# A hybrid decoder layer on one core: two products of four units directly behind the keys, and eight operand sums moved to GpSimd

## The chip, the core and the metric

The kernel runs on one core of a Trainium2 chip. A core has a matrix engine (TensorE, PE in the profile; its weight loads are listed as PEld), VectorE (DVE), ScalarE (ACT), GpSimd (POOL) and SyncE (SP), which issues most DMAs. Each engine runs its own instruction stream in order and waits at semaphores for the others. The metric is the device time of one execution in microseconds (us), as the median of several runs.

## The reference

One layer over 2048 tokens of 1024 channels in fp32. The combined projection `w_in` makes convolution inputs, queries, keys, values and gates; a short causal convolution and a sliding-window attention (16 heads of 64, 4 key heads, window 128) run beside each other, and two gated projections and one last projection follow.

```python
h = rms_norm(x, norm_g)
u = jnp.einsum('bsd,dc->bsc', h, w_in)
v_c, b_c, c_c, z_c, q, k, v, z_a, gate_logits = jnp.split(u, SPLIT_POINTS, axis=-1)
...
y_a = jnp.einsum('bsc,cd->bsd', y_c, w_conv_out)
q = rms_norm(q.reshape(b, s, N_Q_HEADS, HEAD_DIM), q_norm_g)
k = rms_norm(k.reshape(b, s, N_KV_HEADS, HEAD_DIM), k_norm_g)
...
o = sliding_window_attention(q, k, v, sinks) * jax.nn.silu(z_a)
y_b = jnp.einsum('bsc,cd->bsd', o, w_attn_out)
gates = jax.nn.sigmoid(gate_logits + gate_b)
g_a, g_b = jnp.split(gates, N_BRANCHES, axis=-1)
merged = g_a * y_a + g_b * y_b
return x + jnp.einsum('bsd,de->bse', merged, w_out)
```

## The kernel before

**Tiles and units.** The tokens are done in two tiles of 1024, each as two halves of 512. The columns of a projection are done in units of 256 (two blocks of 128). A unit is a 2 x 2 block product (two halves of the channels, two halves of the tokens, two column blocks), and it is computed with seven products instead of eight, after Strassen and Winograd. The products are numbered 1 to 7. Product 1 and 2 use the weights as they are (`_a`), 6 and 5 use sums of them (`_s`), 7 and 3 other sums (`_t`) and 4 the single block `_d`. On the side of the tokens, product m uses the operand m: `form(t, m, j)` makes `oph_m_j`, for each of four chunks j of 128 channels pairs. Operands 5, 6, 7 and 4 are of sums of normed inputs, made by `first_sum`, `third`, `second_sum` and `last_sum`; operands 1, 2, 3 are the normed inputs.

**One product.** fp32 is split in a high and a low part (`split`): ScalarE casts the high part (L306 for operands, L466 for weights), VectorE subtracts it to get the low part (every woven VectorE instruction has line L275). A product is for each of four chunks high x high, high x low and low x high: 12 matmuls 128x512 (L639).

**The opening.** In the first tile the keys and values of all tokens come first (`kv_by_token`, L777, 16 ticks). Behind them, the first gate unit (`ga`, 0) is done by `qunit` with the plain eight products (L754), as its operands 1, 2, 3 and 8 are the normed inputs themselves. Then come the four query units `q` 0 to 3 by `sunit`, the convolution units `cv` and `b`, the rest of the gates, `z`, `za` and the output projections.

In `sunit` product 1 goes to a bank X, ScalarE copies X to the bank Y (L657); product 5 goes to a bank V and is copied to `s5` (L666); product 6 is added on Y, and VectorE makes V = s5 + Y. So the order is 1, 5, 6, 2, 7, 3, 4. `spair` does two units product by product. Finished queries are copied (L790), cast (`q_h`, L1073), stored by four GpSimd DMAs to `q2d` (L1078), and transposed by TensorE for the squares of their norm (`ptq`, L913, squared on ScalarE at L996). Finished gates get a tanh (L1417); finished keys (`k_n`, `ksq`, `kss`, `k_h`) a norm with a square root, whose table ScalarE must load.

**What sets the order.** `manual_schedule` keeps every engine's stream as the program writes it. `run` counts one tick per product; in each tick it writes the next weight piece (high cast first, low part behind), then what `put(n, f)` has noted for tick n, then a few woven VectorE steps. The tables of numbers at the top give these ticks: `OPEN_AT` for the operands of the opening, `KV_PLACES` for keys and values, `STEPS_0` and `STEPS_1` for the steps of attention in the two tiles, `WO_SUMS_AT` for the sums of `w_o` (`wo_sums`), which the last projection reads from DRAM (`wsd`). `plan` lists the weight units in the order of use, with a kind: "S" is a seven-product unit with one load of 1 MB, "P" the eight-product one; `piece` gives out their pieces as room in the weight buffers comes free.

**An attention step** `j_b` (key head j, block b of 128 tokens) has the scores `s_j_b` (the bank is first filled with the sinks by ScalarE, L1237; matmuls L1249 and L1252), a softmax, a turn of p to `f` on VectorE and through DRAM (`fd`, L1293; back as `x`, L1300; both issued by GpSimd), casts to `xh` and `yp` (L1307, L1308), a low part `xl`, four selects on GpSimd (L1321), and the values `po_j_b` (L1338).

Of the kernel before, what the change touches and what calls it, by code (L numbers as in the profile page):

```python
# [8 lines left out]
F32 = mybir.dt.float32  # L9
# [6 lines left out]
P = 128  # L16
# [3 lines left out]
H = 512  # L20
# [37 lines left out]

K_AT = (1, 1, 4)

T0_SHIFT = 1
OPEN_AT = (2, 2, 2, 7, 7, 8, 5, 4, 5, 6, 4, 6, 5, 5, 6, 7, 9, 6, 7, 8, 7, 8, 8, 10, 12, 11, 14, 14, 14, 13, 17, 14, 14, 19, 18, 14, 16, 20, 20, 19, 20, 20, 18, 16, 19, 14, 20, 19, 22, 22, 23, 22, 23, 23, 8, 8, 14, 14, 26, 18, 22, 25, 27, 20, 26, 27, 21, 19, 23, 24, 18, 19, 19, 19, 28, 22, 28, 27)
KV_PLACES = (8, 11, 22, 26, 8, 11, 13, 40, 13, 31, 31, 30, 36, 36)
TURNED_AT = (6, 12)

K_ROOT = True
# [14 lines left out]
STEPS_0 = (60, 63, 71, 74, 78, 85, 92, 95, 99, 104, 110, 115, 121, 128, 131, 136, 139, 142, 146, 149, 152, 155, 159, 162, 165, 170, 173, 176, 181, 184, 187, 192)  # L81
# [44 lines left out]
def block_kernel(  # L126
# [281 lines left out]
    def load_half(i=None):  # L408

        if i is None:
            i = next(k for k in range(2 * len(plan)) if k not in raws)
        n, h = divmod(i, 2)
        kind, srcs, key = plan[n]
        if kind == "L":
            raws[i] = None
            return
        if n not in raw_of:  # L420
            raw_of[n] = rawpool.tile(
                [P, 2, 2, H], F32, tag="raw", name="w" + "_".join(str(i) for i in key) + "_raw")
        both = raw_of[n]
        if kind == "R":
            raw = both[:, h]
            for p in range(2):
                nc.sync.dma_start(raw[:, p], srcs[(2 * h + p) * P : (2 * h + p + 1) * P])

                for c in FIRST_X.get((i, p), ()):
                    xt_load(c, 0)  # L430
        elif kind in "SP":
# [12 lines left out]
        raws[i] = raw  # L444
        rawlive[0] += 1
# [11 lines left out]
    def pieces_of(n):  # L457
# [37 lines left out]
        if kind in "SP":  # L495
            def pair(h, m1, m2, nm):
                hi, lo = (v.rearrange("p (i j c) -> p i j c", i=2, c=P) for v in wpair(f"{name}_{nm}"))
                for i, m in enumerate((m1, m2)):
# [2 lines left out]
                return two(hi, lo, raw[:, h] if summed else raw[:, :, h])  # L501

            summed = []

            if kind == "P":
                return w, [(2, 2 * h, lambda h=h: pair(h, (h, 0), (h, 1), f"p{h}")) for h in range(2)]

            def single():
                hl = wpool.tile([P, 2, KP, P], F32R, tag="w", name=f"{name}_d")
# [38 lines left out]
            def second():  # L548
# [3 lines left out]
                for i, m in enumerate((7, 3)):  # L552
# [25 lines left out]
    def open_prep():  # L578
        n = len(ready)
        if n >= len(plan):  # L580
            return False
        if n in paired:
            both = [pieces_of(n + e) for e in range(2)]
            ready.extend(w for w, _ in both)
            todo.extend((n + e, i) + both[e][1][i] for e, i in (PAIR_LOADS if plan[n][0] == "L" else PAIR_PIECES))
            return True
        w, pieces = pieces_of(n)
        ready.append(w)
        todo.extend((n, i) + p for i, p in enumerate(pieces))
        return True  # L590

    def piece():

        if not todo and (len(ready) > used[0] or not open_prep()):
            return None
        n, i, cost, last, f = todo[0]
        if tick[0] < held.get(n, 0):
            return None
        need = [2 * n + i] if plan[n][0] in "TP" else [2 * n, 2 * n + 1][: 1 + min(i, 1)]
# [30 lines left out]

    B_AT = {(0, 0): 1, (1, 0): 2, (0, 1): 8, (1, 1): 3}

    def product(ps, u, n, ops, start):
        force(u, n)
        hi, lo = ready[u][n]
        for j in range(KP):
            b = ops[n][j]
            for i, (w, m) in enumerate(((hi, 0), (hi, 1), (lo, 0))):
                nc.tensor.matmul(  # L639
                    ps, lhsT=w[:, j, :], rhs=b[:, m, :],  # L640
                    start=start and j == 0 and i == 0, stop=j == KP - 1 and i == 2,
                    skip_group_check=not start)
        d = done.setdefault(u, set())
        d.add(n)
        live[0] -= sum(c for m, c in USES if n in m and m <= d)
# [94 lines left out]
    def qunit(key, ops, fin):  # L740


        u = unit(key)
        nm = "_".join(str(i) for i in key)
        for q in range(2):
            for i in range(2):
                ps = bank(f"Q{nm}_{i}_{q}")
                for p in range(2):
                    force(u, (i, p))
                    hi, lo = ready[u][i, p]  # L750
                    for j in range(KP):
                        b = ops[B_AT[p, q]][j]
                        for k, (w, m) in enumerate(((hi, 0), (hi, 1), (lo, 0))):
                            nc.tensor.matmul(  # L754
                                ps, lhsT=w[:, j, :], rhs=b[:, m, :],
                                start=p == 0 and j == 0 and k == 0, stop=p == 1 and j == KP - 1 and k == 2)
                    if p:
                        fin(i, q, ps)
                        live[0] -= 2 * q
                    yield  # L760

    def kv_by_token(places, banks):

# [84 lines left out]
    def norm_l(t, c, st):  # L848
        x_norm(st["raw"][c, 0], c, st["rb"][0])

    def third(c, st):

        raw = st["raw"]
        sub(raw[c - 1, 1], raw[c, 1], raw[c - 1, 1])

    def norm_r(t, c, st):

# [9 lines left out]
        raw = st["raw"]  # L867
        sub(raw[2 * j, 0], raw[2 * j + 1, 1], raw[2 * j, 0])

    def last_sum(j, st, to=None):  # L870

        raw = st["raw"]
        o = st.setdefault("t4", {})[j] = raw[2 * j, 0] if to is None else to
        sub(o, raw[2 * j + 1, 0], raw[2 * j, 0])

    def form(t, m, j, st):
        raw = st["raw"]
# [754 lines left out]
    for t in range(NT):  # L1632
# [9 lines left out]
        else:  # L1642
            at_(("k", t))
            at_(("v", t))
        for j in range(EARLY[t]):
            at_(("ga", t, j))
        for j in range(NKV):
            at_(("q", t, j))
        if t == 0:
            plan[2] = ("P",) + plan[2][1:]  # L1650
        for k in range(KC):
            at_(("cv", t, k))
            if k % 2:
# [148 lines left out]
    put(OPEN_AT[31], lambda: form(0, 8, 1, st))  # L1802
    put(OPEN_AT[32], lambda: form(0, 8, 2, st))
    put(OPEN_AT[33], lambda: form(0, 8, 3, st))
# [25 lines left out]
    put(OPEN_AT[59], lambda: third(3, st))  # L1830
    put(OPEN_AT[60], lambda: third(5, st))
    put(OPEN_AT[61], lambda: third(7, st))
# [123 lines left out]
    for t in range(NT):  # L1956
# [12 lines left out]
        firsts = [(("ga", t, j), fin_g(t, 0, j)) for j in range(EARLY[t])]  # L1969
        firsts += [(("q", t, j), fin_q(t, j)) for j in range(NKV)]  # L1970
        for n, (key, fin) in enumerate(firsts):
            run((qunit if t == n == 0 else sunit)(key, ops, fin))
        for k in range(KC):
            run(sunit(("cv", t, k), ops, fin_cv(t, k, ys)))
            if k % 2:
# [17 lines left out]
        zs += [("za", j) + fin_z(t, j, od[t], "za", use_y) for j in range(NJ)]  # L1993
        zs[0][3]()
        if t + 1 == NT:
            for j in range(KP):
                wo_sums(tick[0] + WO_SUMS_AT[j], j)
        if t == 0:
            for j in range(2):
# [151 lines left out]
```

## Time and profile before

| | us |
|---|---|
| median of 3 runs | 1901.33 (1898.82 to 1902.93) |
| the profiled execution | 1901.07 |
| its span, first to last instruction | 1899.4 |
| TensorE busy | 1888.9 |
| VectorE busy | 1498.6 |
| ScalarE busy | 990.5 |
| GpSimd busy | 608.7 |

The granted TensorE clock is 1.000 over the whole span. A row of the timeline gives the start, the time that it and what is grouped with it took, engine, line, operation, output and inputs, and in brackets the idle time before it with what ended it; two neighbouring starts on an engine tell what one instruction costs there, since the end of one overlaps the next.

### The profile page before, as it was taken

The page shows a single profiled execution, that of the slowest core. Times are in us where ns is not written, and L with a number is a line of the kernel's source. Part 1 is how long each engine was busy: PE and PEld are TensorE (multiplying, and loading weights), DVE is VectorE, ACT ScalarE, POOL GpSimd, SP SyncE. Part 2 cuts the span into 40 slices and gives each one's busy share as a digit, 9 for nine tenths or more (in the row PEclk, how much of TensorE's full clock was granted, in tenths as well). Part 3 has the DMA queues.
Part 4 walks back from the last instruction along what each step waited for, and adds up shares of the span by engine and source line. Part 5 has one row for each costly group of instructions (what it writes and reads, how often), then busy time and mean ns, then how long its engine had stood idle before and what let it go on. Part 6 is the DMA issues. An engine that isn't in the chain of part 4 may idle for free.

```text
span 1899.4 us, 27260 instructions
## 1 busy us (share of the span) xinstructions
PE 1888.9 (99%) x8670; PEld 1572.7 (83%) x8670; DVE 1498.6 (79%) x2364; ACT 990.5 (52%) x1967; POOL 608.7 (32%) x846
## 2 busy tenths in 40 slices
PE   9999999999999999999999999999999999999999
PEld 7888888888887888888888888888888888888887
DVE  7989898887777767668799788887778777787754
ACT  7665455456766443434565455556666434444321
POOL 2073435335655000011372344445656000121000
PEclk9999999999999999999999999999999999999999
DMA  8286555568777957895584655567778887779653
GB/s 299 77 238 177 167 169 167 162 189 245 240 229 226 302 197 245 276 279 130 155 233 128 181 175 154 168 206 228 242 235 256 272 319 274 274 194 264 215 175 110
DMA packets 222495, 402.20 MB, mean 212 GB/s; under 512 B 30032, under 2 KB 104784, under 8 KB 212880
## 3 DMA queue, kind: packets, MB, share of 16 engines
q1 hardware_dynamic: 188224, 313.10, 50.6%
q0 software_dynamic: 30528, 78.94, 15.7%
q10 hardware_dynamic: 3600, 8.42, 1.3%
q8 instruction: 69, 1.13, 0.2%
q14 instruction: 74, 0.61, 0.1%
HBM read 271.09 MB, written 129.25 MB: 211 GB/s over the span
## 4 chain that ended last, share of the span: by engine, by line
PE 65%; DVE 2%; DMA 2%; issue 0%; ACT 0%; SPq 0%; DVEq 0%; ACTq 0%
PE Y L639 24%; PE ya L1479 4%; PE Vcv L639 2%; PE Xcv L639 2%; PE Xyb L639 2%; PE Vo L639 2%; PE Xo L639 2%; PE Vyb L639 2%; PE Vza L639 2%; PE Xza L639 2%; PE Xz L639 1%; PE Vz L639 1%; PE po L1338 1%; PE Vga L639 1%; PE Xgb L639 1%; PE Vgb L639 1%
## 5 line engine op out<-in xcount | busy, mean ns | idle before, releaser
L1300 POOL DMA_DIRECT2D x<-fd x256 | 140.0, 554 | 127.0 <-DMA fd<-f 58.1
L1274 ACT ACTIVATE p<-s,st,rq 128x129 f32<-128x129 f32 x256 | 114.2, 458 | 33.2 <-DVE st L275 21.2
L1321 POOL TENSOR_SCALAR_AFFINE_SELECT xh<-xh 64x512 fp32r<-64x512 f32 x64 | 61.0, 953 | 151.4 <-DVE xl L275 103.2
L1293 POOL DMA_DIRECT2D fd<-f x64 | 37.0, 578 | 194.3 <-DVE f L275 169.0
L1562 POOL DMA_DIRECT2D mt<-tha x16 | 13.8, 863 | 254.9 <-DVE tha L275 236.2
L639 PE MATMUL Xcv<-oph,wcv_ah 128*128 128x512 f32 x256 | 78.9, 389 | 0.0
L1321 POOL TENSOR_SCALAR_AFFINE_SELECT yp<-xl 64x512 fp32r<-64x512 f32 x64 | 72.3, 1130 | 3.1
L1321 POOL TENSOR_SCALAR_AFFINE_SELECT xl<-xl 64x512 fp32r<-64x512 f32 x64 | 67.7, 1058 | 4.4
L1321 POOL TENSOR_SCALAR_AFFINE_SELECT yp<-yp 64x512 fp32r<-64x512 f32 x64 | 57.8, 903 | 4.2
L275 DVE TENSOR_TENSOR o<-po,o 64x256 f32<-64x256 f32 x128 | 53.5, 418 | 5.0 <-ACT o L1350 4.1
L275 DVE SCALAR_TENSOR_TENSOR y<-u,cols,y 128x512 f32<-128x512 f32 x64 | 53.6, 837 | 3.7 <-ACT y L1387 2.5
L639 PEld LDWEIGHTS Xcv<-oph,wcv_ah 128*128 128x128 f32 x256 | 47.8, 188 | 9.4
L275 DVE TENSOR_TENSOR p<-p,st 128x512 f32<-128x512 f32 x64 | 50.4, 787 | 3.4
L275 DVE STREAM_TRANSPOSE f<-p 128x512 f32<-128x512 f32 x64 | 45.5, 711 | 8.5 <-DMA fd<-f 5.6
L466 ACT CAST wcv_sh<-wcv_raw 128x1024 fp32r<-128x1024 f32 x16 | 16.9, 1054 | 67.1 <-DVE wcv_raw L275 67.1
L1274 ACT ACTIVATION_READ_ACCUMULATOR p<-s,st,rq 128x1 f32 x256 | 51.3, 200 | 0.0
L1249 PEld LDWEIGHTS s<-kq,q 128*128 128x128 f32 x256 | 46.1, 189 | 5.8 <-ACT s L1237 1.8
L1078 POOL DMA_DIRECT2D q2d<-q_h x64 | 44.3, 692 | 18.9 <-ACT q_h L1073 7.7
L1350 ACT COPY o<-po 64x256 f32<-64x256 f32 x128 | 47.1, 368 | 6.0 <-DMA wpd_yb<-wph_yb 2.2
L2052 POOL DMA_DIRECT2D oc<-ocd x12 | 6.5, 545 | 136.1 <-ACT ophc L306 130.1
L639 PE MATMUL Xcv<-oph,wcv_al 128*128 128x512 f32 x128 | 49.9, 390 | 0.0
L1078 POOL DMA_DIRECT2D q2d<-q_l x64 | 44.2, 690 | 14.7 <-DMA q2d<-q_h 7.5
(711 smaller groups left out, 6409.1 us busy)
## 6 DMA issues: line engine op xcount, KB each, us to landing
gd<-th SPq DMA_DIRECT2D x64, 256.0 KB, 2.8
wcv_raw<-in_w_units SPq DMA_DIRECT2D x16, 1024.0 KB, 5.5
q<-q2d SPq DMA_DIRECT2D x64, 256.0 KB, 5.4
v<-vd SPq DMA_DIRECT2D x128, 128.0 KB, 3.5
fd<-f POOLq DMA_DIRECT2D x64, 256.0 KB, 4.2
x<-fd POOLq DMA_DIRECT2D x256, 64.0 KB, 3.5
th<-gd SPq DMA_DIRECT2D x48, 256.0 KB, 5.0
wga_raw<-in_w_units SPq DMA_DIRECT2D x8, 1024.0 KB, 5.4
```

Of the source, the lines that this page charges most:

```text
L275: r = f(*args, **kw)
L466: return (lambda: nc.scalar.copy(hi, src), lambda: vec.tensor_tensor(out=lo, in0=src, in1=hi.bitcast(F32), op=ALU.subtract))
L639: nc.tensor.matmul(ps, lhsT=w[:, j, :], rhs=b[:, m, :], start=start and j == 0 and i == 0, stop=j == KP - 1 and i == 2, skip_group_check=n ...
L1078: nc.gpsimd.dma_start(q2d[t][j][half, q * 2 * HB : (q + 1) * 2 * HB, i, e, :], src[HALVES[e]].bitcast(F32).rearrange("p (b x) -> p b x", x ...
L1249: nc.tensor.matmul(sp[:, h, c, skip : 3 * HD], lhsT=q2[:, h, c, :], rhs=kq[:, 0, keys], start=c == 0, stop=False)
L1274: nc.scalar.activation(out=p[:, i, :], in_=sg[:, i, HD : 3 * HD + 1], func=AF.Exp, bias=st[:, 1, i : i + 1], scale=rv[:, i // 2, i % 2 : i ...
L1293: nc.gpsimd.dma_start(fd, f)
L1300: nc.gpsimd.dma_start(x[QUADS[k]], src[k])
L1321: nc.gpsimd.affine_select(out=d4, in_=s4, pattern=[[0, 2], [-32 * sg, 2], [0, G], [-sg, 32]], compare_op=ALU.is_gt if prev else ALU.is_ge, ...
L1338: nc.tensor.matmul(po[:, cs], lhsT=v2[:, kind + h, :], rhs=xx[:, :, h * HD : (h + 1) * HD], start=n == h == 0, stop=n == 2 and h == 1)
L1350: nc.scalar.copy(ov, pov[oth, :, e])
L1479: nc.tensor.matmul(ps, lhsT=w[:, j, cs], rhs=o[:, m, :], start=n == 0 and i == 0, stop=n == KC - 1 and i == 2)
```

## The change

The gate unit `ga` 0 becomes a seven-product unit, and the first four units are done in two pairs, (q 0, ga 0) and (q 1, q 2). Behind the keys stand products 1 and 2 of both pairs (`hpair`): product 1 of the two, then product 2 of the two. Product 1 is copied to an SBUF slot `head` by ScalarE, and product 2 finishes its quarter of the unit. For these products half of each unit's weights is loaded on its own (kind "F", 512 KB a unit, 2 MB in all). Then come products 5, 6, 7, 3 and 4 of the first pair, one unit beside the other, and of the second pair (`rpair`); `head` is copied to Y again behind product 5. For these the unit's whole 1 MB is loaded (kind "M"), as the sums need it. Query unit 3 follows by `sunit` as before.

Operand 8 is no longer made (four casts, four low parts). `third` and `last_sum` of the first tile, four each, run on GpSimd. Operand 3 is made some ticks later. In the first tile attention step 28 (3_4) is put one tick earlier and step 30 (3_6) one later, with `T0_SHIFT` 0 for 1, since the opening has one tick less. The `w_o` sums of chunks 0 and 1 move from `z` of the second tile to its start.

```diff
-T0_SHIFT = 1
+T0_SHIFT = 0
-WO_SUMS_AT = (8, 17, 26, 35)
+WO_SUMS_AT = (5, 13, 8, 44)
+OPENING = ((("q", 0, 0), ("ga", 0, 0)), (("q", 0, 1), ("q", 0, 2)))
+REST = (5, 6, 7, 3, 4)
+REST_HOLD = 5
...
+        elif kind == "F":
+            raw = both[:, h].rearrange("p k (j c) -> p k j c", c=P)
+            src = w_units[unit_index(srcs[h])].rearrange("r (k h x) -> r k h x", k=2, h=2)[:, :, 0]
+            nc.sync.dma_start(both[:, h], src)
...
+            if kind == "M":
+                return w, [(0, 0, sums_first), (2, 0, first), (2, 0, second), (1, 2, single)]
...
+    def hpair(key, ops, subs):
         u = unit(key)
...
+        for e, (sub, _) in enumerate(subs):
+            nm = "_".join(str(i) for i in sub)
+            xbs.append(bank(f"X{nm}"))
+            product(xbs[e], u, 1, ops, True, (e, 1))
+            heads[sub] = slot([P, H], F32, f"head{nm}")
+            nc.scalar.copy(heads[sub], xbs[e])
+            yield
+        for e, (_, fin) in enumerate(subs):
+            product(xbs[e], u, 2, ops, False, (e, 2))
+            fin(0, 0, xbs[e])
+            yield
...
+    def rpair(keys, ops, fins):
...
+        held[us[1] + 1] = tick[0] + REST_HOLD
...
+        for n, e in ((n, e) for n in REST for e in range(2)):
+            u, fin, nm = us[e], fins[e], nms[e]
+            if n == 5:
+                vb[e] = bank(f"V{nm}")
+                product(vb[e], u, 5, ops, True)
+                s5[e] = spare(f"s5{nm}")
+                nc.scalar.copy(s5[e], vb[e])
+                if e:
+                    yb[e] = mbank(f"Y{nm}").rearrange("p b q -> p (b q)")
+                nc.scalar.copy(yb[e], heads.pop(keys[e]))
+            elif n == 6:
+                product(yb[e], u, 6, ops, False)
+                add(vb[e], s5[e], yb[e])
...
-        last_sum(j, st, slot([P, H], F32, f"t4_{j}"))
+        last_sum(j, st, slot([P, H], F32, f"t4_{j}"), nc.gpsimd)
...
-    put(OPEN_AT[30], lambda: form(0, 8, 0, st))
...
-    put(OPEN_AT[58], lambda: third(1, st))
+    put(OPEN_AT[58], lambda: third(1, st, nc.gpsimd))
...
+        if t + 1 == NT:
+            for j in range(2):
+                wo_sums(tick[0] + WO_SUMS_AT[j], j)
         attention(t, [t0 + n for n in (STEPS_0, STEPS_1)[t]])
...
+            for j, pair in enumerate(subs):
+                run(hpair(("f", j), ops, pair))
+            for pair in subs:
+                run(rpair([k for k, _ in pair], ops, [f for _, f in pair]))
```

**VectorE in the opening.** First VectorE's stream before, about the weights of the first query unit's products 5 and 6 (`wq_0_sl`) and its products 7 and 3 (`wq_0_tl`); names `oph_m_j` are low parts of operands, `xt` and `t` are sums.

```order
L275 TENSOR_TENSOR wq_0_sl<-wq_0_raw,wq_0_sh 128x1024
L275 TENSOR_TENSOR xt_162<-xt_165,xt_162 128x512
L275 TENSOR_TENSOR xt_169<-xt_172,xt_169 128x512
L275 TENSOR_TENSOR oph_6_1_796<-xt_157,oph_6_1_796 128x512
L275 TENSOR_TENSOR xt_162<-xt_165,xt_162 128x512
L275 TENSOR_TENSOR oph_4_1_800<-t_1_718,oph_4_1_800 128x512
L275 TENSOR_TENSOR oph_6_0_822<-xt_150,oph_6_0_822 128x512
L275 TENSOR_TENSOR oph_6_2_825<-xt_162,oph_6_2_825 128x512
L275 TENSOR_TENSOR oph_6_3_828<-xt_169,oph_6_3_828 128x512
L275 TENSOR_TENSOR t_2_831<-xt_165,xt_162 128x512
L275 TENSOR_REDUCE kss_1_803<-ksq_2_804 128x8
L275 TENSOR_TENSOR t_3_852<-xt_172,xt_169 128x512
```
Behind the weights' low part stand five sums and five low parts of operands and one reduce; the next row is `wq_0_tl`. The same place now:

```order
L279 TENSOR_TENSOR wq_0_sl<-wq_0_raw,wq_0_sh 128x1024
L279 TENSOR_TENSOR oph_6_0_831<-xt_150,oph_6_0_831 128x512
L279 TENSOR_TENSOR oph_6_2_834<-xt_162,oph_6_2_834 128x512
L279 TENSOR_TENSOR oph_6_3_837<-xt_169,oph_6_3_837 128x512
L279 TENSOR_REDUCE kss_1_792<-ksq_2_793 128x8
L279 TENSOR_REDUCE qss_0_644<-ptq_0_0_0_798 128x8
L279 SCALAR_TENSOR_TENSOR q_2_0_0_l<-q_2_0_0_t,gqk,q_2_0_0_h 128x512
L279 TENSOR_TENSOR wga_0_sl<-wga_0_raw,wga_0_sh 128x1024
L279 TENSOR_TENSOR wq_0_raw<-wq_0_raw 128x512 x2
L279 TENSOR_REDUCE qss_1_645<-ptq_1_0_0_872 128x8
L279 TENSOR_TENSOR wga_0_raw<-wga_0_raw 128x512
L279 TENSOR_TENSOR wq_0_tl<-wq_0_raw,wq_0_th 128x1024
```
The sums of operands (`xt`, `t`) are gone from here. Low parts of two units' weights (`wq_0`, `wga_0`) and of the query q_2 stand between, with the reduces of the squares.

**ScalarE in the opening.** Its stream now, at the end of the first pair and in front of product 6 of the second pair; `ptq` are squares of queries, `th` gates, `wq_1` and `wq_2` the second pair's weights.

```order
L300 ACT_TABLE_LOAD
L300 ACTIVATE k_1_t<-k_1_ms 128x16
L1465 ACT_TABLE_LOAD
L1465 ACTIVATE th_0_1_1_1028<-th_0_1_1_1028,hbias 128x512
L1465 ACTIVATE th_0_0_1_1103<-Vga_0_904,hbias 128x512
L474 CAST wq_1_sh<-wq_1_raw 128x1024
L1044 ACTIVATE ptq_0_1_1_1112<-ptq_0_1_1_1112 128x512
L838 COPY q_0_1_0_t<-Y 128x512
L474 CAST wq_2_sh<-wq_2_raw 128x1024
L1121 ACTIVATE q_0_0_1_h<-q_0_0_1_t,gqk 128x512
L1465 ACTIVATE th_0_1_0_1161<-Yga_0_919,hbias 128x512
L474 CAST wq_1_th<-wq_1_raw 128x1024
```
The next three rows are a square, the copy `s5q_1` and `Y<-headq_1`, which fills the bank that product 6 of q_1 is added to. Two table loads stand about the keys' root, where before had the load for the root alone and no tanh behind it; the casts of two units' weights alternate.

**GpSimd in the first tile's attention.** The stream before, about the selects of the steps 3_2 and 3_3:

```order
L1321 AFFINE_SELECT xl_3_2_5772<-xl_3_2_5772 64x512
L1293 DMA fd_3_4_5821<-f_3_4_5819 128x512
L1300 DMA x_3_4_5894<-fd_3_4_5821 32x4x128 x4
L1321 AFFINE_SELECT xh_3_3_5886<-xh_3_3_5886 64x512
L1321 AFFINE_SELECT yp_3_3_5888<-yp_3_3_5888 64x512
L1321 AFFINE_SELECT yp_3_3_5888<-xl_3_3_5887 64x512
L1321 AFFINE_SELECT xl_3_3_5887<-xl_3_3_5887 64x512
```
And now:

```order
L1341 DMA fd_3_4_5786<-f_3_4_5784 128x512
L1369 AFFINE_SELECT xh_3_2_5777<-xh_3_2_5777 64x512
L1369 AFFINE_SELECT yp_3_2_5779<-yp_3_2_5779 64x512
L1369 AFFINE_SELECT yp_3_2_5779<-xl_3_2_5778 64x512
L1369 AFFINE_SELECT xl_3_2_5778<-xl_3_2_5778 64x512
L1348 DMA x_3_4_5858<-fd_3_4_5786 32x4x128 x4
L1369 AFFINE_SELECT xh_3_3_5903<-xh_3_3_5903 64x512
L1369 AFFINE_SELECT yp_3_3_5905<-yp_3_3_5905 64x512
L1369 AFFINE_SELECT yp_3_3_5905<-xl_3_3_5904 64x512
L1369 AFFINE_SELECT xl_3_3_5904<-xl_3_3_5904 64x512
```
The store of `fd_3_4` stands ahead of the selects of 3_2, where it stood behind them.

More of the change, by code (lines that the diff above doesn't have):

```diff
@@ L493, in pieces_of, with head @@
                        for i, ms in enumerate(((1, 2), (6, 5), (3, 7), (4,)))]
-        if kind in "SP":
+        if kind == "F":
+            def head(e):
+                hi, lo = (v.rearrange("p (i j c) -> p i j c", i=2, c=P) for v in wpair(f"{name}_{e}"))
+                for i in range(2):
+                    w[e, 1 + i] = (hi[:, i], lo[:, i])
+                return two(hi, lo, raws[2 * n + e])
+            return w, [(2, 1, lambda e=e: head(e)) for e in range(2)]
+        if kind in "SM":
             def pair(h, m1, m2, nm):
@@ L584, in open_prep @@
             ready.extend(w for w, _ in both)
[L585 removed]
+            order = {"L": PAIR_LOADS, "M": REST_PIECES}.get(plan[n][0], PAIR_PIECES)
+            todo.extend((n + e, i) + both[e][1][i] for e, i in order)
             return True
@@ L738, in pair_outs @@
         return sorted([(at_[2], (0, 0)), (at_[7], (1, 1)), (at_[3], (0, 1)), (at_[4], (1, 0))])
-    def qunit(key, ops, fin):
+    heads = {}
+    def hpair(key, ops, subs):
         u = unit(key)
[L744 to L760, printed above, removed]
+        xbs = []
+        for e, (sub, _) in enumerate(subs):
[9 more added lines that the diff above has]
+            yield
@@ new lines, in rpair @@
+    def rpair(keys, ops, fins):
+        us = [unit(key) for key in keys]
+        held[us[1] + 1] = tick[0] + REST_HOLD
+        nms = ["_".join(str(i) for i in key) for key in keys]
+        vb, yb, s5 = [None, None], [Y, None], [None, None]
+        for n, e in ((n, e) for n in REST for e in range(2)):
[11 more added lines that the diff above has]
+                add(vb[e], s5[e], yb[e])
+            elif n == 7:
+                product(yb[e], u, 7, ops, False)
+                fin(1, 1, (yb[e], s5[e]))
+            elif n == 3:
+                product(vb[e], u, 3, ops, False)
+                fin(0, 1, vb[e])
+            else:
+                product(yb[e], u, 4, ops, False)
+                fin(1, 0, yb[e])
+            yield
@@ L1644, in block_kernel @@
             at_(("v", t))
-        for j in range(EARLY[t]):
-            at_(("ga", t, j))
-        for j in range(NKV):
+        if t == 0:
+            for j, subs in enumerate(OPENING):
+                plan.append(("F", subs, ("f", j)))
+            for subs in OPENING:
+                paired.add(len(plan))
+                for key in subs:
+                    plan.append(("M", ((None, 0), (None, P)), key))
+        for j in range(3 if t == 0 else 0, NKV):
             at_(("q", t, j))
-        if t == 0:
-            plan[2] = ("P",) + plan[2][1:]
         for k in range(KC):
@@ L1968, in block_kernel @@
             run(sunit(("v", t), ops, fin_v(t)))
[L1969 to L1972, printed above, removed]
+        if t == 0:
+            subs = [[(key, fin_q(0, key[2]) if key[0] == "q" else fin_g(0, 0, key[2])) for key in keys]
+                    for keys in OPENING]
+            for j, pair in enumerate(subs):
+                run(hpair(("f", j), ops, pair))
+            for pair in subs:
+                run(rpair([k for k, _ in pair], ops, [f for _, f in pair]))
+        for j in range(3 if t == 0 else 0, NKV):
+            run(sunit(("q", t, j), ops, fin_q(t, j)))
         for k in range(KC):
@@ L1995, in block_kernel @@
         if t + 1 == NT:
-            for j in range(KP):
+            for j in range(2, KP):
                 wo_sums(tick[0] + WO_SUMS_AT[j], j)
```

44 lines of the change are left out of this document (22 added, 22 removed).

## Prediction

> **What bounds the kernel now.** I read the page's span and busy shares first, then the waits of TensorE with its timeline around each, then the windows of 20 us over the opening, where the change stands.
>
> ```profile
> span 1899.4 us, 27260 instructions
> ...
> PE 1888.9 (99%) x8670; PEld 1572.7 (83%) x8670; DVE 1498.6 (79%) x2364; ACT 990.5 (52%) x1967; POOL 608.7 (32%) x846
> ```
>
> TensorE is busy 1888.9 of 1899.4 us. So a matmul that goes saves its time, a wait of TensorE that goes saves its length, and work on the other engines costs only what it makes TensorE wait. The four waits that the change's later edits touch are these (the bracket is the idle time and its releaser):
>
> ```profile
> 578.42 0.51 PE L1338 MATMUL po<-yp,v 128*128 128x256 f32 x2 [0.79 <-POOL yp L1321]
> 579.24 0.50 PE L1338 MATMUL po<-xl,v 128*128 128x256 f32 x2 [0.32 <-POOL xl L1321]
> 589.33 0.47 PE L1249 MATMUL s<-kq,q 128*128 128x192 f32 x2 [1.37 <-ACT s L1237]
> 1511.19 3.02 PE L639 MATMUL Y<-oph,wz_d 128*128 128x512 f32 x12 [0.75 <-DVE zs L275]
> ```
>
> The opening is tighter on the helpers. Columns: window, its length, busy time and instructions of PE, PEld, DVE, ACT, POOL, then clock, DMA share, GB/s.
>
> ```profile
> 40.00:60.00 20.00, 20.00 (x91) 16.40 (x90) 19.61 (x36) 11.68 (x23) 7.78 (x14) 1.00 0.50 152
> 60.00:80.00 20.00, 19.92 (x88) 16.18 (x87) 20.00 (x32) 12.88 (x23) 0.00 (x0) 1.00 0.11 40
> 80.00:100.00 20.00, 20.00 (x97) 16.63 (x97) 17.65 (x29) 15.61 (x27) 6.32 (x11) 1.00 0.44 113
> ```
>
> From 60 to 80 us VectorE has no gap and GpSimd does nothing, and still TensorE loses only 0.08 us: every operand comes in time, without much to spare.
>
> **The change part by part.** All of it is set against the profiled execution, 1901.07 us (its span and 1.67 us around it); the median of the runs is 1901.33, so 0.26 above. The sum is made on 1901.07 and not corrected.
>
> *One product fewer.* The first gate unit goes from eight products to seven: 12 matmuls 128x512, one product.
>
> ```profile
> 647.85 2.72 PE Xza L639 x12
> ```
>
> A product takes 2.72 us where nothing waits: **-2.72**. In the removed unit one pair of matmuls, with its weights late, took 0.97 us where its neighbours take 0.61 or 0.62; that wait goes with it: **-0.36**.
>
> ```profile
> 66.74 0.97 PE L754 MATMUL Qga<-oph,wga_p0h 128*128 128x512 f32 x2
> ```
>
> *The late edits.* Attention step 3_4 is put one product earlier, so GpSimd's x_3_4 and with it the four selects of 3_3 stand 2.7 us sooner; the two waits at 578 and 579 (1.11 us) were for these selects. Step 3_6 is put one product later, and the casts xh_3_4 and yp_3_4 stand ahead of its softmax, no longer in front of the copy s_3_7:
>
> ```profile
> 587.83 0.62 ACT L1307 CAST xh<-x 128x512 fp32r<-128x512 f32 x1
> ...
> 589.11 0.17 ACT L1237 COPY s<-sinks 128x4 f32<-128x4 f32 x1
> ```
>
> Without them the copy comes at 587.8, 1.28 earlier; of the 1.37 us wait nearly all goes. At 1511 TensorE waited for zs, which VectorE did behind a sum that waited 4.43 us for a load:
>
> ```profile
> 1509.24 0.69 DVE L275 TENSOR_TENSOR cr<-cr,cr 128x512 f32<-128x512 f32 x1 [4.43 <-DMA cr<-ocd]
> ```
>
> The w_o sums of one chunk, with their loads and stores on SP ahead of that load, now stand at the start of tile 2. I take all four waits as gone: **-3.23** (0.79 + 0.32 + 1.37 + 0.75). The least is nothing; then they only change their name. The moved sums (twice four of 128x512 on VectorE, about 0.6 us each, and the SP traffic with them) lie at the start of tile 2 beside TensorE's steady products and I cost them at nothing; without that cover it is at most one set late, 2.4 us.
>
> *The new opening.* Here the order counts. Durations are read as start to start of neighbours on VectorE:
>
> ```profile
> 48.10 0.74 DVE L275 SCALAR_TENSOR_TENSOR xt<-xt,cols,rb 128x512 f32<-128x512 f32 x1
> 48.76 0.17 DVE L302 SCALAR_TENSOR_TENSOR k_r<-k_t,k_r 128x16 f32<-128x16 f32 x1
> ...
> 71.30 0.68 DVE L275 TENSOR_TENSOR t<-xt,xt 128x512 f32<-128x512 f32 x1
> 71.90 1.22 DVE L275 TENSOR_TENSOR wq_sl<-wq_raw,wq_sh 128x1024 fp32r<-128x1024 f32 x1
> 73.03 1.29 DVE L275 TENSOR_TENSOR xt<-xt,xt 128x512 f32<-128x512 f32 x2
> ...
> 78.45 0.68 DVE L275 TENSOR_REDUCE kss<-ksq 128x8 f32<-128x512 f32 x1
> 79.05 0.68 DVE L275 TENSOR_TENSOR t<-xt,xt 128x512 f32<-128x512 f32 x1
> ```
>
> So 0.66 for a q low part, 0.60 for a sum or low part of 512, 1.13 for one of 1024, 0.60 for a reduce. On ScalarE:
>
> ```profile
> 69.44 0.68 ACT L1417 ACTIVATE th<-Qga,hbias 128x512 f32<-128x512 f32 x1
> 70.03 1.04 ACT L466 CAST wq_sh<-wq_raw 128x1024 fp32r<-128x1024 f32 x1
> 70.97 0.61 ACT L306 CAST oph<-xt 128x512 fp32r<-128x512 f32 x1
> 71.49 0.62 ACT L306 CAST oph<-t 128x512 fp32r<-128x512 f32 x1
> 72.01 0.83 ACT L934 ACTIVATE k_n<-kv,rtok 128x256 f32<-128x256 f32 x2
> 72.87 0.63 ACT L936 ACTIVATE ksq<-k_n 128x512 f32<-128x512 f32 x1
> ...
> 96.17 1.28 ACT L296 ACT_TABLE_LOAD   x1
> 97.47 0.21 ACT L296 ACTIVATE k_t<-k_ms 128x16 f32<-128x16 f32 x1
> 97.59 0.71 ACT L1073 ACTIVATE q_h<-q_t,gqk 128x512 fp32r<-128x512 f32 x1
> 98.20 0.58 ACT L657 COPY Y<-Xq 128x512 f32<-128x512 f32 x1
> 98.72 0.55 ACT L996 ACTIVATE ptq<-ptq 128x512 f32<-128x512 f32 x1
> 99.20 0.71 ACT L1073 ACTIVATE q_h<-q_t,gqk 128x512 fp32r<-128x512 f32 x1
> ```
>
> That is 0.59 for a tanh, 0.94 for a 1024 cast, 0.52 for a 512 cast or a PSUM copy, 0.86 for a pair of k halves, 0.6 for their square, 1.30 for a table load, 0.12 for the small root, 0.61 for a q high part, 0.48 for the square of a transposed q. TensorE begins behind the keys, as before, at 51.74; a transposition of q takes 0.35 and its next product some 0.14 more (97.43 to 100.29 is 2.86):
>
> ```profile
> 51.74 0.63 PE L754 MATMUL Qga<-oph,wga_p0h 128*128 128x512 f32 x2
> ...
> 97.08 0.60 PE L913 MATMUL ptq<-ident,q_t 128*128 128x128 f32 x4
> 97.43 0.71 PE L639 MATMUL Vq<-oph,wq_sh 128*128 128x512 f32 x2
> ...
> 100.29 0.60 PE L913 MATMUL ptq<-ident,q_t 128*128 128x128 f32 x4
> ```
>
> First place: product 7 of q_0. TensorE asks for it after 12 products and two transpositions, at 51.74 + 32.64 + 0.98 = 85.4, or 85.1 if the 0.14 is hidden; I take 85.2. The second product of q_1 ends at 51.74 + 7 x 2.72 + 0.5 = 71.3. ScalarE then has a square, the copy of q_1 (from 71.7), its high part and wq_0_sh, which starts at 72.9 and ends at 74.0. VectorE, in order: wq_0_sl, three operand low parts, two reduces (1.13 + 1.80 + 1.20), to 78.1; q_2's low part 0.66; wga_0_sl 1.13, two sums and a reduce 1.80, a sum 0.60, wq_0_tl 1.13, the last sum of wga_0 0.68, to 84.1. Only then can ScalarE cast wga_0_th (0.94), two operands (1.04), k_3 and its square (1.46), wq_0_d (0.52) and at last oph_7_0 (0.62): 88.7, with 0.1 to TensorE 88.8. **+3.6.** Part of it is met two products earlier, where product 5 of ga_0 waits for wga_0_sl; whoever waits, the sum is the same. The low part of oph_7_0, on VectorE 0.68 behind the cast, is late for the second matmul: **+0.4**.
>
> Second place: product 6 of q_1. From 88.8 TensorE would reach it after product 7 (with the 0.4), seven products and five transpositions: 88.8 + 0.4 + 21.76 + 2.45 = 113.4. On ScalarE, from the end of product 3 of q_0 (98.0): a copy, a cast of k and a q high part 1.65, a table load for the key root, the root, a table load back to tanh 2.72, two tanh 1.18, to 103.7; wq_1_sh 1.04; VectorE wq_1_sl, two key products and wq_2's two sums, 3.6, to 108.4; wq_2_sh 1.04; wq_2_sl, a q low part, a reduce and wq_1's sums, 3.7, to 113.1; ScalarE wq_1_th, a square, s5 and the copy into Y, 2.5, to 115.7. **+2.4**, and the same once more in small for q_2's Y copy behind wq_2_th, **+0.4**. The second table load, 1.30 of this, is one that before didn't have there. Together the opening costs 3.6 + 0.4 + 2.4 + 0.4 = **+6.8**.
>
> *At nothing:* eight sums and four low parts less on VectorE (12 x 0.60), four casts less and four head copies more on ScalarE, 2 MB more of weights: TensorE waits for none of these itself, and the DMA share of 0.50, 0.11 and 0.44 in the three windows leaves room. If that cover fails, a late 1 MB weight stands at the start of a product and costs its lateness.
>
> *Sums on GpSimd.* No row of before shows one. From below a VectorE sum, 0.68 us; from above twice a GpSimd select of 64x512, 2.2:
>
> ```profile
> 243.82 1.07 POOL L1321 TENSOR_SCALAR_AFFINE_SELECT yp<-yp 64x512 fp32r<-64x512 f32 x1
> ```
>
> I take 1.1, the select's. The last of them, xt_150 for oph_7_0, stands behind q_2's four DMAs (VectorE's q_2 low part, 78.8, plus three issues of about 0.7) and two more sums: about 84, four us before ScalarE casts it. It decides nothing up to about 2.3 us a sum. [...]
>
> Sum: 1901.07 - 2.72 - 0.36 - 3.23 + 6.8 = 1901.56; I say **1901.6**.
>
> **The rivals.**
>
> *A, faster: the opening waits for little.* My chain adds up a written order of some 90 VectorE rows; where one link ends 1 us sooner, what follows moves too. For it: before had VectorE full from 60 to 80 us and TensorE lost 0.08. Against: the chain from wq_0_sh to oph_7_0 has no choice in it, and only its start, 72.9, is an estimate from several rows. With 0 to 2 us of waits: 1894.8 to 1896.8, say 1896.
>
> *B, slower: GpSimd's sums slow VectorE.* Two VectorE instructions of one form, the first pair beside an idle GpSimd, the second beside its selects (243.82 above):
>
> ```profile
> 183.31 1.54 DVE L275 SCALAR_TENSOR_TENSOR y<-u,cols,y 128x512 f32<-128x512 f32 x2
> ...
> 242.99 2.42 DVE L275 SCALAR_TENSOR_TENSOR y<-u,cols,y 128x512 f32<-128x512 f32 x2 [0.24 <-ACT y L1387]
> ```
>
> The factor is 1.57. Five of the sums fall between 70 and 84 us, on the first chain: with 1.1 us each VectorE loses 5.5 x (1 - 1/1.57) = 2.0 us there and the time is 1903.6; with 2.0 us each 3.6 us, and the last sum also comes late, 1905.4 or more. So it turns into a loss that can be told from no change (0.2%, 3.8 us, about what a measurement of this kernel can tell) from about 1.9 us a sum. [...]
>
> *C: the late waits stay.* The selects of 3_3 also wait for VectorE's xl_3_3, and zs may wait for another load. Then -3.23 falls away: 1904.8, or 1903 with half.
>
> **How the numbers follow.** Forecast (1898 to 1904.5) 0.50, A 0.27, B 0.13, C 0.10. Faster by over 0.2% is below 1897.5: A and a little of the forecast's lower edge, 0.30. Slower is over 1905.1: most of B and part of C with a longer opening, 0.18. Same 0.52. The range, 1895.0 to 1906.0, takes in A's middle, the sums at 2 us and the loss of the late gains.
>
> **What would show it.** In the profile after: 12 matmuls fewer; waits of TensorE for wga_0_sl, oph_7_0 and the Y copy of q_1, of some 2.6, 1.5 and 2.4 us, between 75 and 120 us; no wait at po_3_3, s_3_7 and wz_3_d; GpSimd's TENSOR_TENSOR near 1.1 us, and VectorE's low parts beside it longer than 0.68. It is wrong if TensorE passes 75 to 120 us with under 2 us idle, or if a late wait of the old kind stands again.

## The result, and the profile after

The changed kernel takes 1931.38 us (median of 4 runs, 1930.42 to 1932.43) against 1900.60 us before: ratio 1.0162, 95% interval 1.015 to 1.0175. It is slower by 30.8 us, where the forecast was 1901.6 us and the range ended at 1906.

The page of the changed kernel, its span and busy shares:

```profile
span 1930.7 us, 27244 instructions
...
PE 1896.5 (98%) x8658; PEld 1577.1 (82%) x8658; DVE 1505.8 (78%) x2363; ACT 993.4 (51%) x1971; POOL 616.7 (32%) x854
```

There are 12 matmuls fewer in the count, and yet TensorE is busy 7.6 us longer. So besides waiting more, its matmuls must run slower somewhere. The six largest of its waits, summed by what released them (us in total, times, longest):

```profile
PE Y L658 <- DVE Vq L279: 11.5, 2, 9.0
PE Vq L658 <- DVE wq_sl L279: 3.4, 2, 3.2
PE Y L658 <- DVE Vz L279: 3.3, 1, 3.3
PE ptq L961 <- ACT q_t L838: 3.0, 2, 2.8
PE Vga L658 <- DVE wga_sl L279: 2.1, 1, 2.1
PE Y L658 <- ACT Y L795: 2.0, 1, 2.0
```

The slow matmuls show in TensorE's timeline, directly behind a wait:

```profile
79.43 0.70 PE L658 MATMUL Vq<-oph,wq_sl 128*128 128x512 f32 x1 [3.19 <-DVE wq_sl L279]
79.92 1.06 PE L658 MATMUL Vq<-oph,wq_sh 128*128 128x512 f32 x2
80.77 0.63 PE L658 MATMUL Vq<-oph,wq_sl 128*128 128x512 f32 x1
81.20 1.06 PE L658 MATMUL Vq<-oph,wq_sh 128*128 128x512 f32 x2
82.05 0.63 PE L658 MATMUL Vq<-oph,wq_sl 128*128 128x512 f32 x1
82.48 0.86 PE L658 MATMUL Vq<-oph,wq_sh 128*128 128x512 f32 x2
83.18 0.40 PE L658 MATMUL Vq<-oph,wq_sl 128*128 128x512 f32 x1
83.41 0.62 PE L658 MATMUL Vga<-oph,wga_sh 128*128 128x512 f32 x2
```

Start to start is 0.43 us a matmul from 79.92 to 82.48, and 0.23 again from about 83. The windows say why (the column behind the five engines is the granted clock of TensorE):

```profile
70.00:79.40 9.40, 6.24 (x30) 4.84 (x28) 9.33 (x12) 9.30 (x17) 5.87 (x9) 1.00 0.39 70
79.40:82.90 3.50, 3.47 (x8) 2.74 (x9) 3.50 (x3) 0.02 (x1) 3.13 (x4) 0.52 0.60 112
```

After 3.2 us of waiting the next 3.5 us run at a granted clock of 0.52.

For the whole span I took, for every matmul, the time to the next start less the median of its form, and summed it by place: lost time against TensorE's own pace. Waits are the gaps over 0.3 us, slow matmuls those at nearly twice their median. (Counted like this, a wait is 0.1 to 0.2 us longer than the idle time that its row shows in brackets; where no row is shown, the text gives this count.)

| place | after, us lost | of which slow matmuls |
|---|---|---|
| 0 to 50 us, loads and first sums | 2.1 | 0.2 |
| 70 to 140, the two pairs | 18.5 | 6.3 |
| 140 to 180, in front of query unit 3 | 4.0 | 0 |
| 659, V of z | 5.1 | 1.6 |
| 988, V of a query unit in tile 2 | 12.0 | 2.4 |
| whole span | 45.0 | 10.5 |

Before, the whole span lost 9.6, with about 1 of slow matmuls. 45.0 - 9.6 less the product saved, 2.7, is 32.7, against 31.3 between the two spans; so this count holds the whole change, and its five places are 41.7 of the 45.0. The four late waits that were to go (578, 579, 589 and 1511) are gone.

VectorE's timeline about GpSimd's sums shows the first cause. GpSimd's sums, then VectorE in the same stretch:

```profile
68.66 1.61 POOL L317 TENSOR_TENSOR t<-xt,xt 128x512 f32<-128x512 f32 x1 [2.50 <-DVE xt L279]
...
73.18 1.30 POOL L317 TENSOR_TENSOR xt<-xt,xt 128x512 f32<-128x512 f32 x1
...
80.60 1.29 POOL L317 TENSOR_TENSOR t<-xt,xt 128x512 f32<-128x512 f32 x1
...
87.36 1.30 POOL L317 TENSOR_TENSOR t<-xt,xt 128x512 f32<-128x512 f32 x1
88.60 2.53 POOL L317 TENSOR_TENSOR xt<-xt,xt 128x512 f32<-128x512 f32 x2
```

```profile
69.04 1.78 DVE L279 SCALAR_TENSOR_TENSOR q_l<-q_t,gqk,q_h 128x512 fp32r<-128x512 f32 x1
...
72.07 2.98 DVE L279 TENSOR_TENSOR xt<-xt,xt 128x512 f32<-128x512 f32 x2
...
79.29 3.76 DVE L279 TENSOR_TENSOR oph<-xt,oph 128x512 fp32r<-128x512 f32 x3
...
87.76 3.92 DVE L279 TENSOR_TENSOR wga_raw<-wga_raw 128x512 f32<-128x512 f32 x1
```

A VectorE row that takes 0.68 by itself took 3.92 across the three GpSimd sums from 87.36 to 91.13: it ended 0.55 us behind the last of them. The row from 69.04 ended 0.55 behind the sum from 68.66, and the two rows from 72.07 ended 0.57 behind the sum from 73.18. Of the three rows from 79.29 the second ended at 82.45, 0.56 behind the sum from 80.60. So the rows here are not stretched by a factor, as I had read them before: VectorE stood until GpSimd's sum had ended and then did its row. The second pair of rival B in the prediction shows the same: it ended at 245.41, 0.52 behind the select from 243.82 to 244.89. In the five places of the opening VectorE stood some 8.6 us.

At 983 us VectorE and SP show another cause: SP comes to the loads `krb` late, because the stores of the moved w_o sums stand in front of them, and VectorE stands at the key product that needs `krb`, with the sum V behind it.

```profile
983.16 0.69 DVE L279 TENSOR_TENSOR k_t<-k_t,krb 128x512 f32<-128x512 f32 x1 [7.45 <-DMA krb<-krd]
```

```profile
963.36 4.49 SPq L1654 DMA_DIRECT2D wsd<-wos  x3
967.95 5.18 SPq L1200 DMA_DIRECT2D krb<-krd  x2
973.22 2.29 SPq L1654 DMA_DIRECT2D wsd<-wos  x1
```

Before, no store stands among these loads, and the last six go out in one row:

```profile
934.57 4.19 SPq L1152 DMA_DIRECT2D krb<-krd  x6
```

Now two of the six are issued from 967.95, the four others from 955.40 on. The slowest of the loads also took 12.7 us to land, for 8.0 before.

At 655 us ScalarE's copy of `o` waited 6.89 us for a store of prepared weights to land, and at 144 us its cast of unit 3's first weights waited for their load:

```profile
655.05 0.75 ACT L1398 COPY o<-po 64x256 f32<-64x256 f32 x2 [6.89 <-DMA wpd_yb<-wph_yb]
...
144.02 1.05 ACT L474 CAST wq_ah<-wq_raw 128x1024 fp32r<-128x1024 f32 x1 [5.28 <-DMA wq_raw<-in_w_units]
```

### The profile page after: what moved, and what is told of

Same layout as the page of the kernel before. It is cut to its first block, busy times and chain, and to the rows that moved or that the text cites. A ratio compares the mean times of both kernels' runs of the same rounds, so it can differ in the third digit from the quotient of the medians.

```text
span 1930.7 us, 27244 instructions
## 1 busy us (share of the span) xinstructions
PE 1896.5 (98%) x8658; PEld 1577.1 (82%) x8658; DVE 1505.8 (78%) x2363; ACT 993.4 (51%) x1971; POOL 616.7 (32%) x854
## 4 chain that ended last, share of the span: by engine, by line
PE 89%; DVE 4%; DMA 4%; issue 1%; ACT 1%; POOL 0%; SPq 0%; DVEq 0%; ACTq 0%; POOLq 0%
PE Y L658 32%; PE Vcv L658 5%; PE Xcv L658 5%; PE ya L1527 4%; PE Vb L658 2%; PE Vgb L658 2%; PE Xgb L658 2%; PE Xga L658 2%; PE Xb L658 2%; PE po L1386 2%; PE Vo L658 2%; PE Xo L658 2%; PE Vyb L658 2%; PE Xyb L658 2%; PE Xza L658 2%; PE Vza L658 2%
```

## The experiments

Two theories stood against each other for the opening. G: VectorE stands still while a GpSimd sum runs. O: the written order is late, whoever does the sums. For the rest each part of the change was undone, or done alone.

**The sums back on VectorE.**

```diff
-        last_sum(j, st, slot([P, H], F32, f"t4_{j}"), nc.gpsimd)
+        last_sum(j, st, slot([P, H], F32, f"t4_{j}"))
...
-    put(OPEN_AT[58], lambda: third(1, st, nc.gpsimd))
+    put(OPEN_AT[58], lambda: third(1, st))
...
```

> The changed kernel with the eight operand sums back on VectorE, nothing else. Theory G (a VectorE instruction with two SBUF inputs makes no headway while a GpSimd sum runs): the eight GpSimd sums go, and with them about 8.5 us of stretched VectorE rows (1.78 for 0.74, 2.98 for 1.3, 3.76 for 1.9, 3.92 for 0.7 and so on); VectorE gets 8 x 0.60 = 4.8 us of work back. TensorE's loss between 70 and 140 us, 18.5 us against its pace, falls to about 10 to 12: 1922 to 1925 us. Rival O (the written order of weight pieces and query parts is what is late, whoever does the sums): the loss stays or grows by the 4.8 us: 1931 to 1936.

1923.03 us, ratio to before 1.0122 (1.0101 to 1.0144): 8.4 us less than the change, inside G's range. With eight more sums on it, VectorE does the same three operand low parts in half the time:

```profile
76.50 1.89 DVE L279 TENSOR_TENSOR oph<-xt,oph 128x512 fp32r<-128x512 f32 x3
```

Between 70 and 140 us the loss is 13.3 us for 18.5. So 5.2 us come back there, less than G named: it had the loss fall to 10 to 12. Another 4.2 us lie at tile 2, where the wait was 4.6 for 9.1 us in this profile. None of the eight sums runs there and that wait differs from run to run, so it can't be credited to the sums. O stays for what is left.

**The sums on GpSimd alone, in the kernel before.**

> The kernel before with nothing changed but that the same eight sums run on GpSimd. Theory G: VectorE, full from 60 to 80 us, loses about 1 us for each sum that falls beside its work and gains 0.6 for each that it no longer does, so a net loss of 2 to 4 us, and TensorE waits in the opening: 1903 to 1908 us. Rival O: VectorE has 4.8 us less to do and nothing is late: 1900 to 1901 us.

1904.35 us, 1.0016 (1.0006 to 1.0025): slower by about 4 us by the medians and by 1 to 5 by the interval, as G has it. Here the blocking also goes the other way. While VectorE ran one row behind the other, two GpSimd sums took 9.51 us, the first of them 8.25; ScalarE, in order, stood at the cast of such a sum, and the tanh behind it held the bank that TensorE needed:

```profile
64.07 9.51 POOL L313 TENSOR_TENSOR t<-xt,xt 128x512 f32<-128x512 f32 x2 [4.48 <-DVE xt L275]
...
77.11 3.27 POOL L313 TENSOR_TENSOR t<-xt,xt 128x512 f32<-128x512 f32 x2 [1.83 <-DVE xt L275]
80.34 3.41 POOL L313 TENSOR_TENSOR xt<-xt,xt 128x512 f32<-128x512 f32 x2
```

```profile
78.73 0.62 ACT L306 CAST oph<-xt 128x512 fp32r<-128x512 f32 x1 [0.76 <-POOL t L313]
79.25 0.68 ACT L1417 ACTIVATE th<-Qga,hbias 128x512 f32<-128x512 f32 x1
```

```profile
79.99 1.22 PE L639 MATMUL Vq<-oph,wq_sh 128*128 128x512 f32 x2 [2.87 <-ACT th L1417]
```

**The w_o sums back at z.**

```diff
-WO_SUMS_AT = (5, 13, 8, 44)
+WO_SUMS_AT = (8, 17, 26, 35)
...
-        if t + 1 == NT:
-            for j in range(2):
-                wo_sums(tick[0] + WO_SUMS_AT[j], j)
...
-            for j in range(2, KP):
+            for j in range(KP):
```

> The changed kernel with the sums of w_o back at z of the second tile, as before. Theory W (at the start of tile 2 SP stands in front of the stores of these sums, so the loads krb of the key norm behind them come late, VectorE waits 7.45 us for krb and TensorE 9.1 for V): the loss of 12 us against the pace about 988 us goes, and the 0.9 us at 1511 comes back: 1920 us. Rival (the shifted opening moves tile 2's keys against their loads): the wait at 988 stays, 1931 to 1932.

1925.89 us, 1.0134 (1.0119 to 1.0149): 5.5 us less. Nothing is left of the wait at 988. The gain is smaller than the 12 us lost there in the profile after; that wait differs between runs (4.6 us with the sums on VectorE, 6.1 with the steps back), and a wait of 1.65 us came at 1587.

**The w_o sums moved alone, in the kernel before.**

> The kernel before with only the sums of w_o of chunks 0 and 1 moved to the start of the second tile, as in the change. Theory W: with the stores of these sums ahead of the loads krb on SP, VectorE waits for krb and TensorE for V at about 960 us, whatever the opening did: 5 to 12 us of waits and slow matmuls there, 0.9 us less at 1511: 1904 to 1911 us. Rival (it only goes wrong behind a late opening): 1899 to 1900 us.

1907.27 us, 1.0035 (1.0022 to 1.0049): about 8 us slower by the medians and 4 to 9 by the interval, so a late opening isn't needed for it. The same place, first VectorE, then TensorE:

```profile
961.37 0.69 DVE L275 TENSOR_TENSOR k_t<-k_t,krb 128x512 f32<-128x512 f32 x1 [6.56 <-DMA krb<-krd]
```

```profile
966.81 1.22 PE L639 MATMUL Y<-oph,wq_th 128*128 128x512 f32 x2 [8.12 <-DVE Vq L275]
```

**The attention steps back.**

```diff
-STEPS_0 = (60, 63, 71, 74, 78, 85, 92, 95, 99, 104, 110, 115, 121, 128, 131, 136, 139, 142, 146, 149, 152, 155, 159, 162, 165, 170, 173, 176, 180, 184, 188, 192)
+STEPS_0 = (60, 63, 71, 74, 78, 85, 92, 95, 99, 104, 110, 115, 121, 128, 131, 136, 139, 142, 146, 149, 152, 155, 159, 162, 165, 170, 173, 176, 181, 184, 187, 192)
```

> The changed kernel with attention steps 3_4 and 3_6 of the first tile at the old ticks. Theory S (the swap freed 578, 579 and 589, but costs the 3.4 us wait for V of z at 658): waits of 1.1 and 1.4 us come back, 5.1 us go: 1929 us. Rival (the wait at 658 comes from the stores of prepared yb weights on SP, not from the swap): it stays and the time is 1934 us.

1928.68 us, 1.0149 (1.0134 to 1.0164): 2.7 us less. The interval overlaps that of the change, but the slowest of these runs, 1929.42, is below the fastest of the change, 1930.42. The wait at 659 is gone and waits of 0.90, 0.48 and 1.75 us stand at the old places.

**Both steps moved alone, and only the first of them, in the kernel before.**

> The kernel before with both steps moved as the change does, and nothing else. If the wait of 3.4 us with 1.6 us of slow matmuls at 659 belongs to 3_6 one tick later: 1900.2 - 3.0 + 5.0 = 1902.2 us, with TensorE waiting for V of z at about 630. Rival (it needs the shifted opening too): 1897 us.

> The kernel before with attention step 3_4 of the first tile one tick earlier and 3_6 where it was. Theory P (3_4 earlier frees the selects of 3_3; it is 3_6 later that holds up SP's store of its od and with it the yb weights): the 1.4 us at 578 and 579 and perhaps the 1.5 at 589 go, nothing comes at 640 to 660: 1897.5 to 1899 us against 1900.2. Rival: the wait at 650 comes with the earlier 3_4: 1902 or more.

With both: 1902.42 us, 1.0015 (1.0006 to 1.0024), slower, with the wait for V of z:

```profile
642.57 1.05 PE L639 MATMUL Y<-oph,wz_th 128*128 128x512 f32 x2 [2.96 <-DVE Vz L275]
```

Its profiled run, 1904.85 us, also has a wait of 1.83 us at 448 with a slow stretch behind it, long before the two steps.

With 3_4 alone: 1896.97 us, 0.9982 (0.9973 to 0.9991). That is 2.7 us faster than before, and the fastest kernel of the study. The waits of TensorE in it are these (us in total, times, longest):

```profile
PE Y L1701 <- DVE zero L197: 1.5, 1, 1.5
PE po L1338 <- DMA gd<-th: 0.6, 1, 0.6
PE Y L639 <- DVE zs L275: 0.5, 1, 0.5
PE kv L777 <- DVE wkv0h L1725: 0.3, 1, 0.3
```

The waits at 578, 579 and 589 are gone with 3_4 alone, the last too. So 3_6 one tick later gives nothing and costs the wait at 659. How, SP's and then ScalarE's timeline of the kernel with both show:

```profile
630.40 0.37 SPq L1358 DMA_DIRECT2D od<-o  x1
630.86 1.86 SPq L339 DMA_DIRECT2D wp_yb<-in_w_units  x4
...
633.25 0.42 SPq L358 DMA_DIRECT2D wpd_yb<-wph_yb  x1
```

```profile
638.71 0.75 ACT L1350 COPY o<-po 64x256 f32<-64x256 f32 x2 [6.59 <-DMA wpd_yb<-wph_yb]
```

SP stands at the store of an attention output, and behind it are the stores of prepared weights whose landing gives ScalarE the buffer for the next `o`. With 3_4 alone this store comes 11.2 us behind the attention store before it, for 15.9 us here, and the copy waits 2.69 us. That the store is 3_6's is read from the order of the steps; it wasn't tried with another place for the store.

**The pairing alone.** The three parts undone together.

> The changed kernel with three parts undone together: the eight sums on VectorE, the sums of w_o at z, steps 3_4 and 3_6 at their old ticks. What is left is the pairing of the first units. If the parts add up (8.3, 5.5 and 2.7 us less in the runs of one part each), 1931.4 - 16.5 = 1914.9 us, so the pairing alone costs some 15 us: 5 to 8 us of waits between 70 and 130 us, 3 us of slow matmuls behind them, and 3 to 4 us about 150 us. Rival (the parts share a cause, the lateness of the opening): more than the sum comes back, 1905 us or less.

1917.24 us, 1.0089 (1.0075 to 1.0102). The parts add up nearly: 14.1 us came back for 16.5. The pairing itself costs 17.6 us by the medians. The profiled run, 1914.01, is the fastest of the four, and its span is 12.9 us longer than before's. In it TensorE still waits 1.40 and 2.54 us in product 5 of q_0 and ga_0, 0.62 and 0.96 in product 7, 2.19 in product 6 of q_1 and 2.96 about 150 us, some 3 us of matmuls are slow, and one product is saved.

**Idle time filled.** In the changed kernel, matmuls whose results are thrown away.

```diff
+FILL = {("q", 0, 0): 10, ("ga", 0, 0): 8}
...
                 vb[e] = bank(f"V{nm}")
+                o = ops[5][1]
+                for _ in range(FILL.get(keys[e], 0)):
+                    nc.tensor.matmul(vb[e], lhsT=o[:, 0, :P], rhs=o[:, 0, :], start=True, stop=True)
                 product(vb[e], u, 5, ops, True)
```

> The changed kernel with matmuls that compute nothing needed in front of product 5 of q_0 (ten) and of ga_0 (eight), into the bank that the product then starts anew; they lie in time in which TensorE waited 3.35 and 2.22 us. Theory C (a wait of over some 2 us makes the next 3.5 us of matmuls run at 0.43 us each for 0.227, whatever was waited for): with the wait cut to about 1.0 and 0.4 us the slow stretches behind the two (1.4 and 1.7 us) go, 1928.5 us. Rival (the slow matmuls come from what else runs then, GpSimd's sums and the DMAs): they stay slow, 1931 to 1933 us.

1927.99 us: with 18 matmuls more it is 3.4 us faster than the change by the medians. The windows, first of the change, then with the idle time filled:

```profile
80.00:85.00 5.00, 4.03 (x12) 2.86 (x10) 5.00 (x6) 1.08 (x2) 2.54 (x3) 0.70 0.51 93
85.00:90.00 5.00, 3.91 (x10) 3.10 (x11) 5.00 (x5) 1.04 (x1) 4.68 (x6) 0.66 0.41 84
```

```profile
80.00:85.00 5.00, 3.75 (x17) 2.77 (x15) 5.00 (x6) 1.08 (x2) 2.23 (x4) 1.00 0.41 82
85.00:90.00 5.00, 4.40 (x19) 3.66 (x20) 5.00 (x5) 2.13 (x3) 4.99 (x6) 1.00 0.42 80
```

GpSimd and the DMAs do nearly the same; the clock is 1.00. As to the clock, theory C stands. As to the time it doesn't: all that was won is given back. The wait in front of product 7 is 4.30 us here for 2.73, since VectorE is no earlier, and from the first product of the opening to product 7 of q_0 it takes 45.35 us for 45.33. To the first product of query unit 3 it is 103.33 for 103.38. The places at 659 and 988 waited less in this profile (2.46 and 3.02 us), which the filling doesn't explain. The gain comes from there, and that the time met the expected 1928.5 was luck.

**Unit 3's first cast later.** The pairing alone, with the hold of the second pair 7 ticks for 5.

> The run with the pairing alone, and the first weight piece of query unit 3 released two ticks later, so that on ScalarE its cast stands behind the copies of q_1 and q_2 and no longer in front of them. Theory L (at 139 us ScalarE stands at that cast for 4 to 5 us, until the 1 MB load has landed, whose buffer came free late, and the copies behind it hold up the transpositions on TensorE): the waits of 0.56 and 2.96 us at 141 and 150 go, and at most 1 us comes back where unit 3 begins: 1914 to 1915 us against 1917.2. Rival (unit 3's weights are late in any case): the wait moves to its first products, 1917 us or more.

1917.15 us for 1917.24: the rival was right. The waits at 141 and 150 are gone, and unit 3 waits for its own weights instead:

```profile
151.26 0.73 PE L658 MATMUL Vq<-oph,wq_sh 128*128 128x512 f32 x2 [1.82 <-ACT wq_sh L474]
```

A pair keeps two buffers of raw weights nearly to its end, and the third unit pays for it in whichever row: in the changed kernel its load goes out at 134.79, 0.07 us behind the last VectorE row that reads the pair's first buffer.

## Why the prediction was wrong, step by step

- *One product fewer, -2.72, and -0.36.* Right: 12 matmuls fewer, and the unit with the late pair is gone.
- *The rows of the new opening, +6.8.* Three places were right, product 5 of ga_0, product 7 of q_0 and product 6 of q_1. The longest wait of the stretch, 3.2 us in product 5 of q_0, was not among them. VectorE came to `wq_0_sl` at 78.15, where the working has 74.0; 1.2 us of this is the opening's start at 52.91 for 51.74, and in the rows before it VectorE had stood 3.5 us for GpSimd's sums. From `wq_0_sl` to the last sum of `wga_0` it then took 15.3 us for the 10.1 of the working, and the two stands in between are 5.1. With the sums on VectorE the waits are 5.6 us at the first place (1.39 and 2.55 in product 5 of the two units, 0.65 and 1.00 in product 7) for the 4.0 forecast, and 2.2 at the second for 2.4. Two more things failed. The low part of `oph_7_0` was named as the last link; TensorE waited for V of q_0, which stands just in front of it on VectorE. And nothing was said of the clock behind a wait: 6.3 us of slow matmuls in this stretch, 10.5 in all. I priced a wait of TensorE at its length; with the four waits of 2.00 to 3.19 us in this stretch TensorE lost those 6.3 us more against its pace, some 1.6 a wait. What that cost the kernel is open, since with two of the waits filled product 7 began no earlier.
- *Sums on GpSimd decide nothing up to 2.3 us a sum.* This was the wrong step of the working. The shortest of them took 1.29 us, where I had taken 1.1 from the select; both are far below 2.3. But I asked when the sums would be ready, and not what VectorE could do meanwhile; in rival B I took a factor of 1.57 from the selects. The rows show VectorE standing in five places, some 8.6 us in all, each time until 0.55 to 0.57 us behind the end of GpSimd's sum. The runs put it at 8.4 us undone, of which 5.2 lie in the opening, and at 4 us done alone.
- *The w_o sums at the start of tile 2, nothing, at most 2.4.* Wrong: about 8 us alone. I counted VectorE's 0.60 us each and did not ask what stands behind the stores on SP, though the prediction names the SP traffic that moves with them: two loads `krb` did.
- *The late edits, -3.23.* The four waits went. But 3_4 alone takes the first three of them; 3_6 later was credited with the copy s_3_7 and instead put 3 to 5 us in front of V of z.
- *Weights at nothing.* Some 3.7 us about 150 us come from the load for unit 3, whose buffer the pair holds; I had priced the loads by the DMA share and not by when a buffer comes free.

By size the pairing was the largest miss. Alone it costs 17.6 us, where -2.72 - 0.36 + 6.8 gives 3.7. In its profiled run the difference to before is 12.9 us, 9.2 more than that: 4.0 about 150 us, some 3 of slow matmuls, 0.9 in the waits that were forecast and 1.0 before the opening begins. Its other runs, 3 to 4 us slower, left no trace. That in the opening it is the written order that is late is read from the rows, and no run changed that order.

Of the rivals, B named a cause that the runs show in the opening, but priced it at 2 to 4 us; its sign was right. The loss of 8 us in tile 2 was in none of them.

## What to carry to other kernels

When a wait of the matmul engine grows to some 2 us, look at the granted clock behind it (here 0.55 from 127.0 to 130.7 us, where a wait of 2.00 had just ended); but before filling the idle time, ask which engine sets the next start, for if that one is no earlier, as here, nothing is won. Don't move sums like these eight to GpSimd beside a full VectorE: alone that cost about 4 us here. When work moves, go through every queue it issues to, and ask what stands behind it there; and undo the parts of a change one by one, since a good one (here 3_4, 2.7 us) can be hidden among bad ones.

## What the runs showed of the hardware

- In the changed kernel five waits of TensorE, of 2.00 to 3.26 us, were followed by matmuls 128x512 at 0.43 us start to start for 0.227. It isn't only the length: one of 2.79 us at 156 was not followed by any in the same profile, and no run tested what sets it apart. The granted clock was 0.50 for 3.41 us from 79.56, 86.39, 100.04, 127.35 and 659.82, 0.13 to 1.80 us behind the ends of the five waits (79.43, 86.09, 98.24, 127.13 and 658.92), and for 10.24 us from 984.09, within the wait of 9.0 us that ended at 988.61; TensorE ran the last 5.7 us of these at half clock. From 155.4 to 158.8 it was 1.00.
- With 18 matmuls whose results are thrown away, in two of the waits, the granted clock was 1.00 in the two windows from 80 to 90 us where it had been 0.70 and 0.66.
- VectorE's low parts and sums of 512 columns went behind GpSimd's sums and not side by side with them: in all five places where such a row met such sums in the changed kernel, it ended 0.55 to 0.57 us behind GpSimd's sum. GpSimd's sums took 1.29 to 1.61 us there; in the kernel before with the sums on GpSimd one took 8.25 us, while VectorE ran row behind row.
